# A 32-row form of an expert's last block in a mixture-of-experts kernel

## Chip, core and metric

The kernel runs on one core of a Trainium2 chip. The metric is the device time of one execution in microseconds (us). Engines are named as in the profile: PE (matmul; PEld is its weight load, PEq or PEldq its instruction sequencer), DVE, ACT, POOL, SP. L1120 is line 1120 of the kernel before.

## What is computed

The reference is a two-layer network in fp32: an RG-LRU mixer with a mixture-of-experts (MoE) layer over 1,280 tokens (1,024 and 256 of context), then a differential attention with a second MoE layer over 1,024 tokens. The change is in the MoE. Each token goes to 2 of 32 experts, and an expert is

```
yb = (silu(x @ w_gate[e]) * (x @ w_up[e])) @ w_down[e]     # 1024 -> 512 -> 1024
out[token] += yb * weight[token]
```

The routing of the drawn inputs gives these tokens per expert, in the order in which the kernel takes the experts. Layer 0: 105, 63, 87, 113, 56, 75, 60, 153, 36, 76, 44, 105, 123, 89, 97, 69, 40, 40, 55, 153, 18, 49, 19, 107, 24, 102, 125, 41, 140, 82, 37, 177. Layer 1: 75, 80, 14, 6, 26, 274, 40, 43, 7, 246, 4, 7, 49, 43, 34, 14, 15, 170, 0, 8, 1, 133, 5, 92, 16, 284, 9, 16, 129, 146, 0, 62. In blocks of 64 rows, with one block at least, that is 54 blocks in each layer.

## The kernel before

`moe` (from L1033) is called once for each layer. An expert's weights are six chunks of 1 MB (two of gate, two of up, two of down), loaded by SP's queue through `load` into a ring of 20 buffers (`raws`); a load waits until PE has read what the buffer held, and is left out where an expert has no tokens (`used`). POOL gathers each block's token rows (`fetch`, `gather`) and scatters the results (`y_out`).

A block of up to 64 rows has four steps on PE. `gate_up` (L1114): 16 fp32 matmuls of 512 columns, two at a time on the two 64-column tiles of the array, one for gate and one for up; the profile shows each as two records, 32 in all. ACT then takes SiLU of the one half, and DVE multiplies it by the other into `hm`. `x_t` (L1109) transposes the rows of the next block through `p_x` into `xt`. `down` (L1131) is the down projection of the block *before*: 8 matmuls (16 records) into `p_y`, which `y_out` scales on ACT into `ym` and scatters from POOL. `h_t` (L1125) transposes this block's `hm` into `ht`. So PE does gate_up of a block, x_t of the next, down of the last and h_t, over and over.

The number of blocks is only known on the chip. `nblk` holds it for each expert (L1023, L1024), and each engine loads it into a register (`count`, L1152). The program is written out for five blocks of each of the 32 experts, one inside the other (`finish`, L1190): `tc.If(n > b + 1)` at L1193 goes into the next block, its Else ends the expert, and the engine jumps past the parts that it doesn't need. This branch stands behind gate_up on every engine. On PE a branch hint (`expect`) is given ahead of gate_up; it names the Else as the likely target. The branch has no other work than the jump, but PE's code must be at hand: a DMA queue (q8 in the profile) brings it in packets of 16 KB.

## Time and profile before

| | us |
|---|---|
| median of 3 runs (lowest, highest) | 3120.76 (3112.51, 3124.94) |
| profiled execution, its span | 3128.07, 3126.5 |
| mean granted clock of TensorE | 0.946 |
| MoE of layer 0 (from 613.7 to 1300.1 us of the span) | 686.4 |
| MoE of layer 1 (from 2358.1 to 3064.1 us) | 706.0 |

The busy time of an engine is the sum of its instructions; a row of a group gives line, engine, operation, the tiles that it writes and reads, and after the bars its busy time, the mean of one and the idle time of the engine just before it, with what ended most of that. "issue" is idle time for which the profile shows no other engine as the cause. The granted clock is a share of 2.4 GHz.

### The profile page before, as it was taken

The page shows a single profiled execution, that of the slowest core. Times are in us where ns is not written, and L with a number is a line of the kernel's source. Part 1 is how long each engine was busy: PE and PEld are TensorE (multiplying, and loading weights), DVE is VectorE, ACT ScalarE, POOL GpSimd, SP SyncE. Part 2 cuts the span into 40 slices and gives each one's busy share as a digit, 9 for nine tenths or more (in the row PEclk, how much of TensorE's full clock was granted, in tenths as well). Part 3 has the DMA queues.
Part 4 walks back from the last instruction along what each step waited for, and adds up shares of the span by engine and source line. Part 5 has one row for each costly group of instructions (what it writes and reads, how often), then busy time and mean ns, then how long its engine had stood idle before and what let it go on. Part 6 is the DMA issues. An engine that isn't in the chain of part 4 may idle for free. (4 is left out here: it accounts for less than half of the span.)

```text
span 3126.5 us, 40919 instructions
## 1 busy us (share of the span) xinstructions
PE 2770.1 (89%) x14542; PEld 1709.2 (55%) x14542; DVE 1374.5 (44%) x2597; ACT 964.4 (31%) x1813; POOL 532.8 (17%) x756
## 2 busy tenths in 40 slices
PE   5999989699999999658999999997977989999991
PEld 3667768433333333257888888886862333333330
DVE  6566676511111111297666666666771111111115
ACT  4566642100011001245454544545420101001011
POOL 2121101211111111140110111100021111112113
PEclk8999989799999999879999999998988999999996
DMA  5556465588879987450000000003255786888544
GB/s 199 160 176 207 161 210 183 195 318 352 342 288 357 377 325 277 149 189 23 26 27 6 26 26 27 6 7 135 105 216 224 313 350 268 346 345 350 196 155 179
DMA packets 175212, 611.49 MB, mean 196 GB/s; under 512 B 28488, under 2 KB 81504, under 8 KB 127104
## 3 DMA queue, kind: packets, MB, share of 16 engines
q1 hardware_dynamic: 133872, 493.85, 41.4%
q0 software_dynamic: 39936, 111.52, 9.9%
q8 instruction: 217, 3.56, 0.5%
q14 instruction: 275, 2.25, 0.2%
q10 hardware_dynamic: 912, 0.32, 0.0%
HBM read 560.23 MB, written 64.22 MB: 200 GB/s over the span
## 5 line engine op out<-in xcount | busy, mean ns | idle before, releaser
L1120 PE MATMUL p_g<-wr,xt 128*64 128x512 f32 x3456 | 775.8, 600 | 40.6 <-ACT ym L1142 32.1
L1120 PEld LDWEIGHTS p_g<-wr,xt 128*64 128x64 f32 x3456 | 268.5, 138 | 465.1 <-issue 413.9
L1123 DVE TENSOR_TENSOR hm<-act,p_g 64x512 f32<-64x512 f32 x108 | 74.7, 692 | 839.7 <-ACT act L1122 804.9
L1136 PE MATMUL p_y<-wr,ht 128*64 128x512 f32 x1728 | 412.6, 610 | 19.4 <-issue 18.1
L1122 ACT ACTIVATE act<-p_g 64x512 f32<-64x512 f32 x108 | 63.6, 589 | 798.2 <-PE p_g L1120 768.5
L1136 PEld LDWEIGHTS p_y<-wr,ht 128*64 128x64 f32 x1728 | 118.6, 138 | 229.2 <-issue 214.2
L56 PE MATMUL qkv<-qwh,hth 128*128 128x384 f32 (+1 forms) x640 | 216.2, 338 | 2.0 <-ACT hth L1439 1.1
L57 PE MATMUL qkv<-qwh,htl 128*128 128x384 f32 (+1 forms) x640 | 210.1, 328 | 0.9 <-DVE htl L1444 0.9
L58 PE MATMUL qkv<-qwl,hth 128*128 128x384 f32 (+1 forms) x640 | 209.4, 327 | 0.6 <-DVE qwl L1294 0.6
L1534 DVE TENSOR_REDUCE st<-sc 128x1 f32<-128x1280 f32 x128 | 190.2, 1486 | 22.0 <-PE sc L1521 20.4
L1129 DVE COPY ht<-p_h 128x256 f32<-128x256 f32 x108 | 45.9, 425 | 342.1 <-PE p_h L1128 336.4
L1537 ACT ACTIVATE wide<-sc,st 128x1280 f32<-128x1280 f32 x128 | 168.9, 1325 | 68.7 <-DVE st L1534 68.6
L1560 PE MATMUL po<-V,wide 128*128 128x128 f32 x1280 | 167.2, 288 | 1.5 <-ACT wide L1554 0.5
L1560 PEld LDWEIGHTS po<-V,wide 128*128 128x128 f32 x1280 | 156.7, 201 | 13.4 <-ACT wide L1554 12.6
L1105 POOL DMA_INDIRECT wide<-h2d,tabs x108 | 112.2, 1039 | 280.8 <-issue 79.6
L1554 ACT COPY wide<-wtp 128x512 f32<-128x512 f32 (+1 forms) x192 | 87.8, 522 | 199.9 <-PE wtp L1553 199.7
L1566 POOL DMA_DIRECT2D od<-ot x56 | 30.4, 542 | 625.2 <-ACT ot L1563 625.2
L1142 ACT ACTIVATE ym<-p_y,cur 128x512 f32<-128x512 f32 x64 | 44.0, 688 | 285.0 <-PE p_y L1136 233.5
L1518 PE MATMUL sc<-KT,QS 128*128 128x512 f32 (+1 forms) x384 | 117.2, 393 | 15.3 <-ACT KT L1368 11.8
L1112 PEld LDWEIGHTS p_x<-ident,wide 128*128 128x128 f32 x432 | 60.9, 210 | 122.9 <-issue 97.8
L1144 POOL DMA_INDIRECT yd<-ym,tabs x44 | 44.0, 1000 | 491.0 <-POOLq L1193 309.4
L56 PE MATMUL o<-wh,sth 128*128 128x512 f32 x288 | 118.9, 413 | 7.4 <-DVE xres L810 5.1
(354 smaller groups left out, 4652.7 us busy)
## 6 DMA issues: line engine op xcount, KB each, us to landing
wr<-in_moe_w_gate_dram SPq DMA_DIRECT2D x124, 1024.0 KB
wr<-in_moe_w_up_dram SPq DMA_DIRECT2D x124, 1024.0 KB
wr<-in_moe_w_down_dram SPq DMA_DIRECT2D x124, 1024.0 KB
wm<-in_w_mod_dram POOLq DMA_DIRECT2D x80, 512.0 KB
cy<-yd SPq DMA_DIRECT2D x26, 512.0 KB
qraw<-in_da_w_qkv_dram SPq DMA_DIRECT2D x48, 256.0 KB
xd<-xres POOLq DMA_DIRECT2D x18, 512.0 KB
h2d<-h POOLq DMA_DIRECT2D x18, 512.0 KB
```

Of the source, the lines that this page charges most:

```text
L56: nc.tensor.matmul(ps, lh, rh, start=start, stop=False)
L57: nc.tensor.matmul(ps, ll, rh, start=False, stop=False)
L58: nc.tensor.matmul(ps, lh, rl, start=False, stop=stop)
L1105: nc.gpsimd.indirect_dma_start(out=dst, out_offset=None, in_=h2v, in_offset=bass.IndirectOffsetOnAxis(ap=idx, axis=0), bounds_check=2 * N ...
L1120: nc.tensor.matmul(p_g[i * B:(i + 1) * B, :], xt[:, j, h * B:(h + 1) * B], w[i][:, j, :], start=(h == 0 and j == 0), stop=(h == 1 and j == ...
L1123: nc.vector.tensor_tensor(hm[B:], act[B:], p_g[B:], OP.mult)
L1136: nc.tensor.matmul(p_y[h * B:(h + 1) * B, :], ht[:, 2 * c + j, :], w[:, j, h * 512:h * 512 + 512], start=(c == 0 and j == 0), stop=(c == 1 ...
L1518: nc.tensor.matmul(o, qs[:, half, :], KT[b][:, half, c0:c0 + n], start=True, stop=False)
L1534: nc.vector.tensor_reduce(st[:, half:half + 1], sc_[:, half, :], AX.X, OP.max)
L1537: nc.scalar.activation(p, sc_[:, half, :], AF.Exp, bias=st[:, 2 + half:3 + half], scale=0.125, accum_out=st[:, 4 + half:5 + half])
L1554: nc.scalar.copy(wT[:, g * 4:g * 4 + n, :], pt[:, 0:n, :])
L1560: nc.tensor.matmul(po[:, 0:P], wT[:, k, :], V[h % 2][:, k, :], start=(k == 0), stop=(k == TT - 1))
```

## The change

An expert's rows are now counted in quarters of 32 (`nq`, at least one: `n1`), and where their number is odd and at most ten, the last block holds only 32 rows (`odd`). In front of each block's gate_up stands a new branch, `full`; its Else takes the quarter:

- `gate_up_q`: 32 matmuls of 256 columns with 32 rows each, four at a time on the four 32-column tiles of the array (two for gate, two for up). The moving columns are taken as pairs, 8 of every 16 bytes.
- `h_t_q`: two transposes in the place of four.
- `down_q`: 16 matmuls of 256 columns on four tiles; it runs inside the *next* expert's first block, behind a branch on `odds[e]`, with `down` in the other arm (`give`).
- `cur_q`: eight small operations of POOL in the place of one copy; `y_out` then scatters 128 rows of 1 KB.

The old branch, `more`, stands behind the full gate_up as before. The hint for the next `full` is given in `turn`, and the hint for `more` at the head of the full arm. By the counts above, 36 of the 108 blocks become quarters: 12 in layer 0 (3 of experts with one block, 6 with two, 3 with three) and 24 in layer 1 (16 with one block, two of them without tokens; 3 with two, 3 with three, 2 with five).

```diff
-        nc.vector.tensor_scalar(nblk, ct[:, :E], float(B - 1), None, op0=OP.add)
-        nc.vector.tensor_scalar(nblk, nblk, 6, None, op0=OP.arith_shift_right)
+
+        nq, n1, odd, nb = (nblk[:, i, :] for i in range(4))
+        nc.vector.tensor_scalar(nq, ct[:, :E], float(Q - 1), None, op0=OP.add)
+        nc.vector.tensor_scalar(nq, nq, 5, None, op0=OP.arith_shift_right)
+        nc.vector.tensor_scalar(n1, nq, 1.0, None, op0=OP.max)
+        nc.vector.tensor_scalar(nb, n1, 1.0, None, op0=OP.add)
+        nc.vector.tensor_scalar(odd, nb, 1, None, op0=OP.arith_shift_right)
+        nc.vector.tensor_scalar(nb, odd, 1.0, None, op0=OP.mult)
+        nc.vector.scalar_tensor_tensor(odd, odd, 2.0, n1, op0=OP.mult, op1=OP.subtract)
+        nc.vector.scalar_tensor_tensor(odd, n1, 2.0 * NB64 + 0.5, odd, op0=OP.is_lt, op1=OP.mult)
...
+        def gate_up_q(e):
+
+            for h in range(2):
+                w = [chunk(e, 2 * i + h, 4).rearrange("p j (q f) -> p j q f", f=4) for i in range(2)]
+                for j in range(4):
+                    for i in range(2):
+                        for c in range(2):
+                            o = slice((2 * i + c) * Q, (2 * i + c + 1) * Q)
+                            nc.tensor.matmul(p_g[o, 0:2 * P].rearrange("t (q f) -> t q f", f=2),
+                                             xt[:, j, h * B:h * B + Q], w[i][:, j, :, 2 * c:2 * c + 2],
+                                             start=(h == 0 and j == 0), stop=(h == 1 and j == 3),
+                                             tile_position=(0, (2 * i + c) * Q))
+            nc.scalar.activation(act[B:, 0:2 * P], p_g[:B, 0:2 * P], AF.Silu)
+            nc.vector.tensor_tensor(hm[B:, 0:2 * P], act[B:, 0:2 * P], p_g[B:, 0:2 * P], OP.mult)
+
+        def h_t_q():
+            hv = hm[B:, 0:2 * P].rearrange("t (q f) -> t f q", f=2)
+            for f in range(2):
+                nc.tensor.transpose(p_h[:, f, :], hv[:, f, :], ident[B:, B:])
+            nc.vector.tensor_copy(ht.rearrange("p (c f) b -> p f c b", f=2)[:, :, :, 0:Q],
+                                  p_h[:, 0:2, :].rearrange("p f (c r) -> p f c r", r=Q))
+
+        def down_q(e):
+            for c in range(2):
+                w = chunk(e, 4 + c, 2)
+                for j in range(2):
+                    for m in range(4):
+                        nc.tensor.matmul(p_y[m * Q:(m + 1) * Q, 0:2 * P], ht[:, 2 * c + j, 0:Q],
+                                         w[:, j, m * 2 * P:(m + 1) * 2 * P], start=(c == 0 and j == 0),
+                                         stop=(c == 1 and j == 1), tile_position=(0, m * Q))
+
+        def cur_q(cur, t):
+
+            for h in range(2):
+                for s in range(2):
+                    dst = cur[h * B + s * Q:h * B + (s + 1) * Q]
+                    frm = t[h * B:h * B + Q]
+                    nc.gpsimd.tensor_scalar(dst[:, 1:2], frm[:, 1:2], 2.0, float(s), op0=OP.mult, op1=OP.add)
+                    nc.gpsimd.tensor_copy(dst[:, 2:3], frm[:, 2:3])
...
-        def y_out(cur):
-            ym = yms[len(scat) % 2]
-            nc.scalar.activation(ym, p_y, AF.Copy, scale=cur[:, 2:3].bitcast(F32))
+        def y_out(cur, quarter=False):
+            n = 2 * P if quarter else F
+            ym = yms[len(scat) % 2][:, 0:n]
+            nc.scalar.activation(ym, p_y[:, 0:n], AF.Copy, scale=cur[:, 2:3].bitcast(F32))
             nc.gpsimd.memset(spacer, 0.0)
-            si = nc.gpsimd.indirect_dma_start(out=ydv, out_offset=bass.IndirectOffsetOnAxis(ap=cur[:, 1:2], axis=0),
-                                              in_=ym, in_offset=None, bounds_check=4 * N - 1, oob_is_err=False)
+            si = nc.gpsimd.indirect_dma_start(out=ydq if quarter else ydv,
+                                              out_offset=bass.IndirectOffsetOnAxis(ap=cur[:, 1:2], axis=0),
+                                              in_=ym, in_offset=None, bounds_check=(8 if quarter else 4) * N - 1,
+                                              oob_is_err=False)
...
-        def turn(xb, e, cur):
-
+        def give(e, cur, quarter):
+
+            if e < 0:
+                return
+            if quarter is None:
+                with tc.If(odds[e] > 0) as one:
+                    down_q(e)
+                    y_out(cur, True)
+                with one.Else():
+                    down(e)
+                    y_out(cur)
+            else:
+                down(e)
+                y_out(cur)
+
+        def turn(xb, e, cur, quarter, nxt=None):
+
+            if nxt is not None:
+                expect("full", *nxt)
             if xb is not None:
                 x_t(xb)
-            if e >= 0:
-                down(e)
-                y_out(cur)
-            h_t()
-
-        def expect(e, b):
-
-            tc.mark_branch_hint_location(f"more{l}_{e}_{b}", "LikelyTaken",
-                                         (mybir.EngineType.PE,))
-
-        def finish(e, b, prev):
+            give(e, cur, quarter)
+
+        def expect(what, e, b):
+
+            tc.mark_branch_hint_location(f"{what}{l}_{e}_{b}", "LikelyTaken", (mybir.EngineType.PE,))
+        def block(e, b, prev):
...
+            then = (e + 1, 0) if e + 1 < E else None
+            with tc.If(n > 2 * b + 1, label=f"full{l}_{e}_{b}") as full:
+                expect("more", e, b)
+                gate_up(e)
+                with tc.If(n > 2 * b + 2, label=f"more{l}_{e}_{b}") as more:
+                    if b + 1 < NB64:
+                        if b + 2 < NB64:
+                            fetch(e, b + 2)
+                        turn(rows_of(e, b + 1), *prev, (e, b + 1))
+                        h_t()
+                        block(e, b + 1, (e, tab(e, b), False))
...
+                with more.Else():
+                    turn(nxt, *prev, then)
+                    h_t()
+                    nc.gpsimd.tensor_copy(curs[e % 2], tab(e, b))
+            with full.Else():
+                gate_up_q(e)
+                turn(nxt, *prev, then)
+                h_t_q()
+                cur_q(curs[e % 2], tab(e, b))
...
-            n = count(ORDER[e])
+            n = count(ORDER[e], 1)
+            odds[e] = count(ORDER[e], 2)
             know(e + 5)
-            expect(e, 0)
-            gate_up(e)
             fetch(e + 1, 1)
             fetch(e + 2, 0)
-            finish(e, 0, (e - 1, curs[(e - 1) % 2]))
+            block(e, 0, (e - 1, curs[(e - 1) % 2], None))
             for k in ([] if e == 0 else [6 * e - 2, 6 * e - 1]) + list(range(6 * e, 6 * e + 4)):
                 load(k + NM)
-        down(E - 1)
-        y_out(curs[(E - 1) % 2])
+        give(E - 1, curs[(E - 1) % 2], None)
```

How this moves PE's instructions shows at two places. The first is the seam between an expert's last block and the next expert's gate_up, in layer 0. Before (`p_h` is h_t, `nblk` the load of the block count, `p_g` gate_up; a TENSOR_LOAD is the register load):

```order
L1128 MATMUL p_h<-ident,hm 128x64 [waits DVE_49]
L1128 MATMUL p_h<-ident,hm 128x64 x3
L1193 UNCONDITIONAL_BRANCH [waits PE_sequencer_49]
L1173 UNCONDITIONAL_BRANCH
L1739 BRANCH_PREFETCH_HINT
L1093 UNCONDITIONAL_BRANCH x4
L1152 TENSOR_LOAD nblk
L1120 MATMUL p_g<-wr_4647,xt 64x512 [waits DMAHW4_49,DVE_49,Activation_49]
```

The same seam now, behind the quarter arm of the expert before it (L1143 is gate_up_q, L1122 x_t, L1153 h_t_q, L1130 gate_up, L1260 the branch `full`):

```order
L1153 MATMUL p_h<-ident,hm 128x64 [waits DVE_49]
L1153 MATMUL p_h<-ident,hm 128x64
L1260 UNCONDITIONAL_BRANCH [waits PE_sequencer_49]
L1226 UNCONDITIONAL_BRANCH
L1103 UNCONDITIONAL_BRANCH x4
L1205 TENSOR_LOAD nblk x2
L1260 COMPARE_AND_BRANCH
L1814 BRANCH_PREFETCH_HINT
L1130 MATMUL p_g<-wr_4653,xt 64x512 [waits DMAHW4_49,DVE_49,Activation_49]
```

A second register load and the `full` branch now stand between an expert's last transposes and the next gate_up, and the hint ahead of gate_up is now that of `more`.

The second place is the quarter arm of the second expert of layer 0, at its head (the first row ends the arm before it; the hint is that of the next expert's `full`):

```order
L1263 UNCONDITIONAL_BRANCH [waits PE_sequencer_49]
L1814 BRANCH_PREFETCH_HINT
L1143 MATMUL p_g<-wr_4653,xt 32x256 [waits DVE_49,DMAHW4_49,Activation_49]
L1143 MATMUL p_g<-wr_4653,xt 32x256
L1143 MATMUL p_g<-wr_4654,xt 32x256 [waits DMAHW5_49]
```

and further on in it, where x_t is followed by both forms of down (L1234 is the branch on `odds`, L1162 down_q, L1186 down):

```order
L1122 MATMUL p_x<-ident,wide_89 128x128 x3
L1234 COMPARE_AND_BRANCH
L1162 MATMUL p_y<-wr_3237,ht 32x256 [waits DMAHW0_49]
L1162 MATMUL p_y<-wr_3237,ht 32x256 x7
L1162 MATMUL p_y<-wr_3238,ht 32x256 [waits DMAHW1_49]
L1162 MATMUL p_y<-wr_3238,ht 32x256 x7
L1234 UNCONDITIONAL_BRANCH
L1186 MATMUL p_y<-wr_3237,ht 64x512 [waits DMAHW0_49]
```

The hint has moved to the head of the quarter arm, right behind the place to which `full` jumps, and each of the three ways out of an expert's first gate_up carries both forms of down. Over the whole program PE's rows grow from 19336 to 29972.

## Rows read from the trace of the kernel before

**Rows 1.** The page: the span, and busy time by engine.
```profile
span 3126.5 us, 40919 instructions
...
PE 2770.1 (89%) x14542; PEld 1709.2 (55%) x14542; DVE 1374.5 (44%) x2597; ACT 964.4 (31%) x1813; POOL 532.8 (17%) x756
```

**Rows 2.** Busy time by stretch: the two MoE stages; columns as in the first line.
```profile
core 0: us, PE busy (x) PEld busy (x) DVE busy (x) ACT busy (x) POOL busy (x), PEclk, DMA share, GB/s
...
613.70:1300.10 686.40, 654.35 (x3020) 251.76 (x3020) 97.11 (x162) 69.75 (x109) 117.11 (x190) 0.99 0.79 309
...
2358.10:3064.10 706.00, 663.66 (x3020) 254.36 (x3020) 96.97 (x161) 69.65 (x109) 116.89 (x190) 0.98 0.72 283
```

**Rows 3.** The page's costliest groups: gate_up and down; count, busy us, mean ns.
```profile
L1120 PE MATMUL p_g<-wr,xt 128*64 128x512 f32 x3456 | 775.8, 600 | 40.6 <-ACT ym L1142 32.1
...
L1136 PE MATMUL p_y<-wr,ht 128*64 128x512 f32 x1728 | 412.6, 610 | 19.4 <-issue 18.1
```

**Rows 4.** Timeline of PE, layer 1, single-block experts: start, us, group, idle before.
```profile
2427.54 7.09 PE L1120 MATMUL p_g<-wr,xt 128*64 128x512 f32 x32 [0.56 <-ACT ym L1142]
2434.55 0.75 PE L1112 MATMUL p_x<-ident,wide 128*128 128x128 f32 x4
2435.24 3.65 PE L1136 MATMUL p_y<-wr,ht 128*64 128x512 f32 x16
2438.82 0.69 PE L1128 MATMUL p_h<-ident,hm 64*128 64x64 f32 x4
2440.08 7.09 PE L1120 MATMUL p_g<-wr,xt 128*64 128x512 f32 x32 [0.56 <-ACT ym L1142]
2447.09 0.75 PE L1112 MATMUL p_x<-ident,wide 128*128 128x128 f32 x4
```

**Rows 5.** Waits of the weight queue (SP), layer 1: total us, times, longest.
```profile
SPq L684 <- PE p_y L1136: 384.4, 47, 53.3
```

**Rows 6.** Timeline of PE around 406 us: a matmul on four 32-column tiles.
```profile
406.09 1.07 PE L147 MATMUL mps<-wm,cs 128*32 128x256 f32 x16
407.09 0.39 PE L56 MATMUL ps_y<-hth,wh 128*128 128x256 f32 x1
```

**Rows 7.** The page's groups: PE's weight loads with contiguous columns, and with every fourth column.
```profile
L1560 PEld LDWEIGHTS po<-V,wide 128*128 128x128 f32 x1280 | 156.7, 201 | 13.4 <-ACT wide L1554 12.6
...
L1112 PEld LDWEIGHTS p_x<-ident,wide 128*128 128x128 f32 x432 | 60.9, 210 | 122.9 <-issue 97.8
```

**Rows 8.** Busy time by stretch, where the DMA engines are full (columns as in Rows 2).
```profile
2425.00:2470.00 45.00, 43.31 (x206) 17.12 (x204) 5.85 (x10) 4.52 (x7) 11.19 (x17) 1.00 1.02 411
```

**Rows 9.** Lines 1024 and 1220: a block-count operation and the copy of cur.
```profile
L1024 DVE TENSOR_SCALAR nblk<-nblk x2: 181/181/181, 599.0 to 2346.2; 128x32 int32<-128x32 int32 x2
...
L1220 POOL COPY cur<-tabs x64: 187/202/235, 639.2 to 3061.4; 128x3 int32<-128x3 int32 x64
```

**Rows 10.** Line 1152, 2436 to 2437 us: the block count loaded for that expert.
```profile
L1152 PEldq TENSOR_LOAD <-nblk x1: 309/309/309, 2436.3 to 2436.3; - x1
```

**Rows 11.** Line 1193, PE's sequencer: compare-and-branch, ns min/median/max, whole run.
```profile
L1193 PEldq COMPARE_BRANCH  x136: 69/302/5992, 618.8 to 3051.3; - x136
```

**Rows 12.** Line 1193, 2442 to 2443 us: one branch of a single-block expert.
```profile
L1193 PEldq COMPARE_BRANCH  x1: 3467/3467/3467, 2442.7 to 2442.7; - x1
```

**Rows 13.** DMA, 2423 to 2461 us: the queue that brings PE's code; packets, MB, share.
```profile
q8 instruction: 6, 0.10, 1.1%
```

**Rows 14.** Line 1193, 668 to 669 us: last branch of a two-block expert.
```profile
L1193 PEldq COMPARE_BRANCH  x1: 332/332/332, 668.6 to 668.6; - x1
```

**Rows 15.** Timeline of PE, layer 0, 645 to 653 us: a stop inside down.
```profile
645.94 1.93 PE L1136 MATMUL p_y<-wr,ht 128*64 128x512 f32 x6
650.12 2.73 PE L1136 MATMUL p_y<-wr,ht 128*64 128x512 f32 x10 [2.25 <-issue]
```

**Rows 16.** Waits of PE, layer 1: total us, times, longest.
```profile
PE p_y L1136 <- issue: 10.7, 4, 2.8
PE p_x L1112 <- issue: 7.6, 6, 5.1
```

More of the change, by code (lines that the diff above doesn't have):

```diff
@@ L46 @@
 B = P // 2
+Q = P // 4
 NB64 = 5
@@ L96, in model @@
     nc.vector.tensor_scalar(ie, ie.bitcast(I32), 1.0 / 64.0, None, op0=OP.mult)
-    nblk = const.tile([P, E], I32, name="nblk")
+    nblk = const.tile([P, 4, E], I32, name="nblk")
     wide = [const.tile([P, UO], F32, name=f"wide{i}") for i in range(3)]
@@ L1072, in moe @@
         rows = {}
+        odds = {}
         h2v = h2d[l][0:N, :].rearrange("n (h d) -> (n h) d", h=2)
-        ydv = yd[l][0:2 * N, :].rearrange("n (h d) -> (n h) d", h=2)
+        ydv, ydq = (yd[l][0:2 * N, :].rearrange("n (h d) -> (n h) d", h=h) for h in (2, 4))
         def tab_load(j0, j1, queues):
@@ L1148, in y_out, with count @@
             scat.append(si)
-        def count(e, engines=None):
+        def count(e, what, engines=None):
             kw = {} if engines is None else {"engines": engines}
-            return nc.values_load(nblk[0:1, e:e + 1], min_val=0, max_val=N // B,
+            return nc.values_load(nblk[0:1, what, e:e + 1], min_val=0, max_val=N // (B if what == 3 else Q),
                                   skip_runtime_bounds_check_because="an expert has at most N tokens", **kw)
@@ L1157, in know @@
             if e < E:
-                used[e] = count(ORDER[e], (mybir.EngineType.SP,))
-                rows[e] = count(ORDER[e], (mybir.EngineType.Pool,))
+                used[e] = count(ORDER[e], 0, (mybir.EngineType.SP,))
+                rows[e] = count(ORDER[e], 3, (mybir.EngineType.Pool,))
         def tab(e, b):
@@ new lines, in turn @@
+            give(e, cur, quarter)
+        def expect(what, e, b):
+            tc.mark_branch_hint_location(f"{what}{l}_{e}_{b}", "LikelyTaken", (mybir.EngineType.PE,))
+        def block(e, b, prev):
+            nxt = rows_of(e + 1, 0) if e + 1 < E else None
+            then = (e + 1, 0) if e + 1 < E else None
[9 more added lines that the diff above has]
+                        block(e, b + 1, (e, tab(e, b), False))
+                    else:
+                        turn(None, *prev)
+                        h_t()
+                        nc.gpsimd.tensor_copy(curs[2], tab(e, b))
+                        with tc.For_i(NB64, count(ORDER[e], 3), 1) as j:
+                            for h in range(2):
+                                nc.gpsimd.dma_start(flat[h * B:(h + 1) * B, 0, :], slotd[l][0:E * N, :].rearrange(
+                                    "(j p e) c -> j p e c", e=E, p=B)[bass.ds(j, 1), :, ORDER[e], :].rearrange(
+                                        "o p c -> (o p) c"))
+                            halve(flat)
+                            gather(xms[0], flat[:, 0, 0:1])
+                            x_t(xms[0])
+                            gate_up(e)
+                            give(e, curs[2], False)
+                            h_t()
+                            nc.gpsimd.tensor_copy(curs[2], flat[:, 0, :])
+                        if nxt is not None:
+                            x_t(nxt)
+                        nc.gpsimd.tensor_copy(curs[e % 2], curs[2])
+                with more.Else():
+                    turn(nxt, *prev, then)
+                    h_t()
+                    nc.gpsimd.tensor_copy(curs[e % 2], tab(e, b))
[4 more added lines that the diff above has]
+                cur_q(curs[e % 2], tab(e, b))
```

28 lines of the change are left out of this document (removed).

## Prediction

> **What bounds the kernel now.** I read the busy times first. PE is busy for 89% of the span [rows 1], and in the two MoE stages for 654 of 686 us and 664 of 706 us, at a granted clock of 0.99 and 0.98 of 2.4 GHz [rows 2]. The groups say with what: gate_up holds 776 us and down 413 us of the whole span [rows 3]. The 3456 records of gate_up are 32 for each of 108 blocks. The timeline then shows one block: gate_up begins at 2427.54, x_t at 2434.55, down at 2435.24, h_t at 2438.82, the next gate_up at 2440.08 [rows 4]. That is 7.01 + 0.69 + 3.58 + 0.69 us, and 0.56 us of waiting at a new expert: 12.54 us. The next candidate is the weight traffic. The DMA engines are busy at a share of 0.79 and 0.72 in these stages [rows 2], but SP, which starts the loads, waits 384 us in layer 1 for PE to release buffers [rows 5]: weights are early, PE is late. So what PE saves in the MoE shortens the kernel until the weights, or something behind them, come last.
>
> **Term 1, the quarter's matmuls.** gate_up's 32 records run two at a time: 16 pairs in 7.01 us, 0.438 us for a pair of 512 columns. gate_up_q has 64 records of 256 columns, 16 sets of four. If four tiles run together at the same column rate, a set takes 0.219 us and gate_up_q 3.5 us. The trace has such matmuls elsewhere: 16 records with 128x32 weights and 256 columns start at 406.09 and the next matmul at 407.09 [rows 6], so four sets in 1.00 us, 0.25 us each, its ends included; by that gate_up_q takes 4.0 us. It saves 3.0 to 3.5 us. down_q has 8 sets, 1.75 to 2.0 us against 3.58, and saves 1.6 to 1.8. Two transposes in the place of four save 0.3. In all 4.9 to 5.6 us for each quarter; I take 5.3, towards the first rate, since 64 records have fewer ends than 16. Times 36 quarters: **191 us** (176 to 202), 64 of it in layer 0.
>
> gate_up_q reads its columns as 8 of every 16 bytes. No row shows a matmul that does so. The nearest is a weight load: of every fourth column, for x_t, it takes 210 ns, of contiguous columns 201 ns [rows 7]. I take it as free; the other end is half the rate, 3.5 us for each quarter, and is a rival below.
>
> **Term 2, the weights.** Where the DMA engines are full they move 411 GB/s [rows 8]. Six chunks are 6.29 MB, 15.3 us. A single-block expert takes 12.54 us of PE now and 7.2 with a quarter, so a run of such experts lives on the ring's 20 buffers, 3.3 experts. Walking the list of experts with 11.9 us for a full block, 6.6 for a quarter and 2.55 us for a chunk, layer 0 never runs dry, and layer 1 (16 of its quarters are alone in their expert) waits some 15 to 25 us in all: **+20 us**.
>
> **Term 3, the small work.** `nblk` takes seven more DVE operations for each layer at 0.18 us [rows 9], ahead of everything that reads a count: **+2 us**. cur_q's eight operations at the 0.2 us of today's copy [rows 9] are 1.4 us more of POOL for each quarter. `cur` is only read when the next expert's down has ended, at least a gate_up and a down later (5 us), and POOL is busy 117 of 686 us [rows 2]: nothing; uncovered it would be 1.4 x 36 = 50 us. The shorter SiLU and product hide under x_t and down as today. The second register load costs PE's sequencer 0.31 us an expert [rows 10]. It is covered: the load at 2436.3 stands ahead of a gate_up that starts at 2440.08, so the sequencer is 3.8 us ahead of PE there. Without that cover it is 64 x 0.31 = 20 us.
>
> **Term 4, the branches.** This is the term that decides, and the trace of before doesn't show it directly. PE's 136 branches at line 1193 take 69 ns to 5992 ns, with a median of 302 [rows 11]. In the single-block expert above, the branch at 2442.7 took 3467 ns [rows 12] although a hint stood 6.4 us in front of it, beside the load at 2436.3 [rows 10]. It cost nothing: it stands behind gate_up, the sequencer had run ahead, and x_t began at 2447.09, right where gate_up ended [rows 4]. Three such experts in a row fetch six packets of code in 38 us [rows 13], two for each expert, one in 6.3 us. In a two-block expert, whose hint comes a whole block earlier, the last branch took 332 ns [rows 14]. And when the code runs on into a packet that isn't there, PE stops in the middle of down for 2.25 us [rows 15]; layer 1 has such stops of 10.7 us in p_y and 7.6 us in p_x [rows 16].
>
> The Trainium skill, "Runtime: NRT & Kernel Launch", section "Instruction fetch mechanics", says that a taken branch to a target outside the sequencer's current two-page window has to wait for that page to be fetched, and that this makes runtime control flow expensive. The 3467 ns agree, the 332 ns after an early hint don't. By that rule alone each jump into or past a quarter arm is a stall, and the sum below would go to its dear end.
>
> The change moves the decision to where there is the least cover: `full` stands *ahead* of gate_up, behind the last transposes of the block before, and its Else lies behind five nested blocks. The hint for it stands at the head of a quarter arm, right behind a jump, when the queue is still busy with the arm's own code.
>
> - 19 quarters that are alone in their expert: a jump of 3.5 us [rows 12] to 6.0 us [rows 11] against a lead of 3.8 us less the extra load after a full block, perhaps half that after a quarter, whose matmuls last half as long. Visible: 1 us to all of the 5.3 us saved, where two packets for each expert at 6.3 us apiece hold it to the old 12.5 us. I take 3.2, nearer to the miss than to the hit, since the rows of single-block experts show misses: +61 us.
> - 17 quarters behind full blocks: the hint comes a block ahead, which is the row of 332 ns, but the arm's second half is new code [rows 15] and the way out jumps past the arms of the blocks around it. 0 to 4 us, I take 2 (about one stop as in rows 15): +34 us.
> - 28 experts whose last block is full: `more` is covered by gate_up as today, but the end now jumps over the quarter's code. 0 to 3 us, I take 1: +28 us.
>
> Together **+123 us** (19 to 253). Some of it falls into layer 1's waits for weights and isn't paid twice: **-15 us**.
>
> **The sum.** 3128 - 191 + 20 + 2 + 123 - 15 = 3067 us for the profiled execution, which lay 7 us above the median of the runs shown: **3060 us**, 2% faster. A measurement of this kernel can tell about 0.5% (16 us) from no change.
>
> **The rivals.**
> - *The hints work everywhere, the branches are hidden.* For it: the 332 ns. Against: single-block experts miss today with a hint some 6 us ahead. Term 4 falls to about 30 us, with less of it under the weights' waits: 3128 - 191 + 20 + 2 + 30 - 5, less 7, gives 2977 us.
> - *Code fetch eats the gain: slower.* One mechanism, at the `full` branch and the arms behind it: each expert needs two or three packets where two came in 12.5 us, and PE stands at the seam until they are there. The gain without branches is 191 - 20 - 2 = 169 us over 64 experts, so it decides where they lose more than 2.6 us on average. With 3.3 us (a 3.5 us miss that is hardly covered) it is 211 us, some 15 under weights' waits: 3128 - 169 + 211 - 15, less 7, gives 3148 us. For it: the 6.3 us of a packet and the stops in down. The rule of "Runtime: NRT & Kernel Launch" in term 4 points this way. Against: full blocks still give cover, and they are the majority.
> - *The quarter isn't half as long*: columns in pairs, or four tiles that don't overlap, give 3.5 us for each quarter back (126 us). A longer quarter hides about a third of term 4 (40 us) and term 2's 20: 3060 + 126 - 60 = 3126 us. Against it: rows 6 and 7.
> - *The weights become the bound of layer 1*: the ring is emptied more often than by my walk, +40 us, 3100 us.
>
> **How the numbers follow.** My forecast has 0.56, the hidden branches 0.16, the slower case 0.17, the longer quarter 0.06, the weights 0.05. My forecast's own range is 3010 to 3110, by term 4 between 70 and 175 us. The range of 8 in 10 takes in most of the first rival and part of the second: 2975 to 3145. Faster by over 0.5% means below 3105: 0.52 of the forecast, the hidden branches and most of the weights: 0.71. Within 0.5%: 0.04 of the forecast, most of the longer quarter and the lower part of the slow case: 0.12. Slower: 0.17.
>
> **What would show it.** In the profile after, gate_up_q should take 3.5 to 4.0 us from its start to x_t (7 would be the third rival), and down_q 1.75 to 2.0. The `full` branch of PE should show a bimodal time, a few hundred ns or 3.5 to 6 us, with the idle time in front of gate_up and gate_up_q; if nearly all are short, the first rival holds. The queue of PE's code should carry more packets than two for each expert [rows 13]. The stages should shrink by 20 to 40 us each; layer 1's, with twice the quarters, not by twice layer 0's. SP's wait for PE should fall, and PE should wait for weights in layer 1 alone. I am wrong if the stage times move while the branches are all short, or if PE's granted clock falls where it waits, of which the stages of before show nothing at 0.98 and more.

## The result: 5% slower, and the profile after

The changed kernel takes 3279.22 us in the median (3271.66 to 3279.32, 4 runs) against 3122.85 us for the kernel before on the same chip: a ratio of 1.0496 (95% interval 1.0474 to 1.0519). I had forecast 3060 us, 2% faster. The page of the changed kernel (line 1130 is now gate_up, 1143 gate_up_q, 1186 down, 1162 down_q, 1122 x_t):

```profile
span 3277.7 us, 46026 instructions
...
PE 2676.6 (82%) x16198; PEld 1715.5 (52%) x16198; DVE 1362.3 (42%) x2609; ACT 949.4 (29%) x1813; POOL 577.0 (18%) x1008
...
q8 instruction: 282, 4.62, 0.6%
...
L1130 PE MATMUL p_g<-wr,xt 128*64 128x512 f32 x2304 | 550.4, 629 | 85.4 <-issue 58.5
...
L1143 PE MATMUL p_g<-wr,xt 128*32 128x256 f32 x2304 | 167.4, 443 | 99.3 <-issue 82.5
...
L1122 PE MATMUL p_x<-ident,wide 128*128 128x128 f32 x432 | 87.2, 328 | 135.8 <-DMA wide<-h2d,tabs 100.8
```

PE's busy share fell from 89% [rows 1] to 82%. The 36 quarters are there: 2304 records of gate_up_q are 64 for each. But the idle time in front of PE's groups is 85 us for gate_up, 99 us for gate_up_q and 136 us for x_t. Of the last, 101 us are waits for gathered token rows; the kernel before had 23 us of them, in two stops at the heads of the stages. By stretch, the two MoE stages (columns as in rows 2):

```profile
608.00:1379.50 771.50, 632.58 (x3576) 256.93 (x3576) 92.93 (x163) 64.62 (x109) 133.31 (x276) 0.91 0.72 276
2439.90:3215.20 775.30, 591.69 (x4128) 253.63 (x4128) 87.96 (x162) 59.50 (x109) 147.09 (x360) 0.87 0.66 259
```

They answer to [rows 2]. The stages took 686 and 706 us and take 772 and 775: the whole loss lies in them. PE is busy 22 and 72 us less, where I had worked out 64 and 127, and the granted clock fell from 0.99 and 0.98 to 0.91 and 0.87. So there are three things to explain: stops of PE for code ("issue"), waits for rows, and a lower clock.

A stretch of layer 1 shows all three. Its experts have one quarter each (timeline of PE, and the granted clock, the last but two number, in one down_q):

```profile
2499.03 3.89 PE L1143 MATMUL p_g<-wr,xt 128*32 128x256 f32 x64 [0.58 <-DVE ht L1154]
2509.82 1.13 PE L1122 MATMUL p_x<-ident,wide 128*128 128x128 f32 x4 [6.91 <-DMA wide<-h2d,tabs]
2510.88 3.64 PE L1162 MATMUL p_y<-wr,ht 128*32 128x256 f32 x32
2514.45 0.45 PE L1153 MATMUL p_h<-ident,hm 64*128 64x64 f32 x2
2516.61 3.90 PE L1143 MATMUL p_g<-wr,xt 128*32 128x256 f32 x64 [1.70 <-issue]
2528.04 1.13 PE L1122 MATMUL p_x<-ident,wide 128*128 128x128 f32 x4 [7.53 <-DMA wide<-h2d,tabs]
```

```profile
2510.90:2514.40 3.50, 3.50 (x33) 1.36 (x32) 0.69 (x1) 0.00 (x0) 0.00 (x0) 0.50 1.01 414
```

gate_up_q takes 3.9 us, as worked out. But from one x_t to the next are 18.2 us, where a whole 64-row expert took 12.54 [rows 4], and after a stop of 6.9 us down_q runs at a granted clock of 0.50, the level of 1.2 GHz, and takes 3.64 us instead of the 1.93 of an undisturbed one (run 1 below). POOL in the same stretch:

```profile
2501.86 1.10 POOL L1115 DMA_INDIRECT wide<-h2d,tabs  x1 [4.14 <-PE p_g L1143]
2507.10 0.09 POOL L1194 MEMSET spacer<- 1x1 f32 x1 [4.14 <-issue]
2508.56 1.02 POOL L1195 DMA_INDIRECT yd<-ym,cur  x1 [1.37 <-DMA yd<-ym,tabs]
2509.65 0.18 POOL L1172 TENSOR_SCALAR cur<-tabs 32x1 int32<-32x1 int32 x1
...
2510.16 0.18 POOL L1173 COPY cur<-tabs 32x1 int32<-32x1 int32 x1
2515.95 0.19 POOL L1172 TENSOR_SCALAR cur<-tabs 32x1 int32<-32x1 int32 x1 [5.61 <-POOLq L1260]
...
2516.68 0.18 POOL L1173 COPY cur<-tabs 32x1 int32<-32x1 int32 x1
2520.80 1.10 POOL L1115 DMA_INDIRECT wide<-h2d,tabs  x1 [3.94 <-PE p_g L1143]
```

cur_q's first four operations follow the scatter of 2508.56. The fifth starts only at 2515.95, some 7.4 us after that scatter was issued, and the next gather only at 2520.80. The profile names POOL's own sequencer as what ended this wait (POOLq L1260). But in the order of POOL's instructions the fifth operation carries a wait for all eight semaphores of POOL's DMAs, that of the scatter just issued among them, in some 190 of the program's 320 quarter arms, and for most of the eight in the others. The gather lands at about 2528, and x_t waits for it. Before, the copy of `cur` waited for two of these at most. POOL is also idle for 4 us behind the jump into a new arm ("issue", the row of 2507.10), though its branches themselves take some 40 ns. In front of these `spacer` operations such stops are 182 us in 62 places; before they were 95 us in 33. POOL seems to wait for its code as PE does; no run tries that apart.

**Theory P** is this chain: POOL's wait for the scatter, the late gather, PE's wait for rows. **Theory F** is code fetch on the sequencers: jumps at seams, arms that push the code apart, and the new branches. Its signs are there too: the queue of code carries 282 packets (217 before), and single passes of the branch `full` take as long as I had expected of a miss, though most are short (line 1260, PE's sequencer; ns min/median/max):

```profile
L1260 PEldq COMPARE_BRANCH  x125: 69/81/6105, 609.1 to 3193.9; - x125
```

### The profile page after: what moved, and what is told of

It reads as the page before. It is cut to its first block, busy times and chain, and to the rows that moved or that the text cites. A ratio compares the mean times of both kernels' runs of the same rounds, so it can differ in the third digit from the quotient of the medians.

```text
span 3277.7 us, 46026 instructions
## 1 busy us (share of the span) xinstructions
PE 2676.6 (82%) x16198; PEld 1715.5 (52%) x16198; DVE 1362.3 (42%) x2609; ACT 949.4 (29%) x1813; POOL 577.0 (18%) x1008
## 5 line engine op out<-in xcount | busy, mean ns | idle before, releaser
L1130 PE MATMUL p_g<-wr,xt 128*64 128x512 f32 x2304 | 550.4, 629 | 85.4 <-issue 58.5
L1130 PEld LDWEIGHTS p_g<-wr,xt 128*64 128x64 f32 x2304 | 187.0, 144 | 393.6 <-issue 362.7
L1133 DVE TENSOR_TENSOR hm<-act,p_g 64x512 f32<-64x512 f32 x72 | 49.8, 692 | 652.6 <-ACT act L1132 628.3
L1186 PE MATMUL p_y<-wr,ht 128*64 128x512 f32 x1152 | 283.8, 638 | 22.9 <-issue 11.6
L1143 PE MATMUL p_g<-wr,xt 128*32 128x256 f32 x2304 | 167.4, 443 | 99.3 <-issue 82.5
L1132 ACT ACTIVATE act<-p_g 64x512 f32<-64x512 f32 x72 | 42.4, 589 | 558.1 <-PE p_g L1130 545.9
L1122 PE MATMUL p_x<-ident,wide 128*128 128x128 f32 x432 | 87.2, 328 | 135.8 <-DMA wide<-h2d,tabs 100.8
L1122 PEld LDWEIGHTS p_x<-ident,wide 128*128 128x128 f32 x432 | 63.1, 210 | 211.2 <-issue 140.6
L1143 PEld LDWEIGHTS p_g<-wr,xt 128*32 128x32 f32 x2304 | 87.0, 122 | 165.2 <-issue 130.6
L1186 PEld LDWEIGHTS p_y<-wr,ht 128*64 128x64 f32 x1152 | 82.4, 145 | 171.6 <-issue 160.1
L1193 ACT ACTIVATE ym<-p_y,cur 128x256 f32<-128x256 f32 (+1 forms) x64 | 36.3, 568 | 408.5 <-PE p_y L1186 124.8
```

What stands on the lines that cost most here:

```text
L1122: nc.tensor.transpose(p_x[:, j, :], xv[:, j, :], ident)
L1130: nc.tensor.matmul(p_g[i * B:(i + 1) * B, :], xt[:, j, h * B:(h + 1) * B], w[i][:, j, :], start=(h == 0 and j == 0), stop=(h == 1 and j == ...
L1143: nc.tensor.matmul(p_g[o, 0:2 * P].rearrange("t (q f) -> t q f", f=2), xt[:, j, h * B:h * B + Q], w[i][:, j, :, 2 * c:2 * c + 2], start=(h ...
L1186: nc.tensor.matmul(p_y[h * B:(h + 1) * B, :], ht[:, 2 * c + j, :], w[:, j, h * 512:h * 512 + 512], start=(c == 0 and j == 0), stop=(c == 1 ...
```

## The experiments

Each ratio is against the kernel before, run on the same chip, with its 95% interval.

**1. cur_q on DVE.**

```diff
-                    nc.gpsimd.tensor_scalar(dst[:, 1:2], frm[:, 1:2], 2.0, float(s), op0=OP.mult, op1=OP.add)
-                    nc.gpsimd.tensor_copy(dst[:, 2:3], frm[:, 2:3])
+                    nc.vector.tensor_scalar(dst[:, 1:2], frm[:, 1:2], 2.0, float(s), op0=OP.mult, op1=OP.add)
+                    nc.vector.tensor_copy(dst[:, 2:3], frm[:, 2:3])
```

> cur_q's eight small operations move from POOL to DVE; nothing else changes. Theory P (POOL's chain): after the change the fifth of these operations waits for the scatter issued just before it, so POOL issues the next gather some 7 us late and PE waits 101 us for gathered rows in x_t. Then this wait falls below 30 us here, most of it in layer 1, and the time falls from 3279 to 3170-3215 us, ratio to the kernel before 1.015-1.03. Theory F (code fetch on PE's and POOL's sequencers alone): the rows come earlier, but PE then stands at its own jumps; the time stays above 3230 us, ratio 1.035-1.05.

3195.61 us, 1.0222 (1.0205 to 1.0239). Theory P's numbers came: x_t waits 23 us for rows in place of 101, as before the change (waits of PE: total, times, longest; first before, then the changed kernel, then this one):

```profile
PE p_x L1112 <- DMA wide<-h2d,tabs: 23.2, 2, 13.0
...
PE p_x L1122 <- DMA wide<-h2d,tabs: 100.8, 22, 13.1
...
PE p_x L1122 <- DMA wide<-h2d,tabs: 23.0, 2, 12.9
```

Layer 0, with few lone quarters, didn't move; layer 1 did (by stretch, columns as in rows 2):

```profile
611.60:1385.20 773.60, 632.84 (x3576) 257.18 (x3576) 102.42 (x259) 64.53 (x109) 115.70 (x180) 0.91 0.71 276
2441.50:3139.10 697.60, 567.37 (x4128) 246.40 (x4128) 107.36 (x354) 59.41 (x109) 112.75 (x168) 0.91 0.74 288
```

POOL's wait is worth 1.0496 - 1.0222 = 0.027, 86 us. That is net of a small new wait: gate_up and gate_up_q stand 24 us for cur_q on DVE. What is left, I put down to theory F. The same experts as above, timeline of PE:

```profile
2507.64 0.75 PE L1122 MATMUL p_x<-ident,wide 128*128 128x128 f32 x4
2508.32 1.93 PE L1162 MATMUL p_y<-wr,ht 128*32 128x256 f32 x32
2510.19 0.44 PE L1153 MATMUL p_h<-ident,hm 64*128 64x64 f32 x2
2515.57 5.81 PE L1143 MATMUL p_g<-wr,xt 128*32 128x256 f32 x64 [4.93 <-issue]
```

x_t now follows at once, and the stop has moved to the seam: 4.93 us for the jump of `full`, and behind it a gate_up_q of 5.81 us where 3.8 would do, at a granted clock of 0.63.

**2. No quarter is ever taken.**

```diff
+        nc.vector.tensor_scalar(n1, nb, 2.0, None, op0=OP.mult)
         nc.vector.scalar_tensor_tensor(odd, odd, 2.0, n1, op0=OP.mult, op1=OP.subtract)
```

> The number of quarters is rounded up to an even one, so no expert ever takes a quarter arm; all branches, hints and arms of the change stay in the program and 108 full blocks run as before the change. Theory F in the form 'a larger program and later hints cost all experts': ratio to the kernel before 1.015-1.04 (about 1-2 us for each of 64 experts), with PE idle as issue in p_g and p_x. Theory F in the form 'only the jumps into quarter arms cost', and theory P (cur_q is never run): 1.000-1.008.

3314.34 us, 1.0625 (1.0595 to 1.0655), more than either form had allowed: the branches and arms cost 195 us though nothing ever jumps into a quarter. Where, from this kernel's profile (gate_up is its line 1131, the branch `more` its line 1264; first the page's group, then PE's passes of line 1264 from 2640 to 2684 us, then the packets of code from 2642 to 2704 us):

```profile
L1131 PE MATMUL p_g<-wr,xt 128*64 128x512 f32 x3456 | 822.3, 626 | 152.9 <-issue 120.5
```

```profile
L1264 PEldq COMPARE_BRANCH  x7: 506/1792/3586, 2642.0 to 2681.3; - x7
```

```profile
q8 instruction: 11, 0.18, 1.2%
```

gate_up waits 120.5 us as "issue"; of the 40.6 us in front of it before, 32.1 were ACT's [rows 3]. Two of line 1264's passes belong to each expert: the branch behind gate_up, and the jump past the quarter arm at its end. The stretch holds some four experts with one full block each, and 11 packets are nearly three for each, where the kernel before took two [rows 13]. That is one packet in 5.6 us, against one in 6.3 before. It isn't the most that the queue can bring: in the same run five came within 20 us (3228.9 to 3249.1).

**3 and 4. The arms chosen when the kernel is built,** from the known counts, with cur_q on POOL and on DVE. This is no kernel for other inputs; it shows the matmuls without branches.

```diff
-            with tc.If(n > 2 * b + 1, label=f"full{l}_{e}_{b}") as full:
+            if last_q(e) == b:
+                gate_up_q(e)
+                turn(nxt, *prev)
+                h_t_q()
+                cur_q(curs[e % 2], tab(e, b))
+                return
```

> The arms are chosen when the kernel is built, from the known token counts: a quarter's arm stands there without the branches full and odds, the blocks that would follow it are not in the program, and full blocks keep the branch more with its hint ahead of gate_up. cur_q stays on POOL. Theory F: all lost time was fetch, so the whole gain of the matmuls appears: 2945-2985 us, ratio 0.945-0.957. Theory P: where cur_q still waits for the scatter, x_t waits for rows; 2990-3060 us, ratio 0.96-0.98. If four tiles or columns in pairs were slow: gate_up_q 7 us and a ratio near 0.98 without waits.

> As the kernel with arms chosen at build time, and cur_q on DVE. Both theories: neither far jumps nor POOL's wait are left, so this is the ceiling of the idea: 2930-2975 us, ratio 0.94-0.953, PE busy in the two MoE stages down by about 190 us, granted clock above 0.95, and weights the only wait of layer 1 (15-25 us). A ratio above 0.97 would say that a third cause, the weights or the clock, holds the gain back.

2995.6 us, 0.9588 (0.9572 to 0.9604), and 2934.45 us, 0.9398 (0.9382 to 0.9414). The first lies between what the two theories expected; the second, at the very edge of its range, is 191 us below the kernel before. The 61 us between them are POOL's wait again: x_t waits 91 us for rows in the first and 27 in the second. By stretch, the second, and its wait for weights in layer 1:

```profile
610.30:1234.70 624.40, 590.66 (x3576) 243.87 (x3576) 102.81 (x259) 64.64 (x109) 115.82 (x180) 0.99 0.86 339
2290.00:2869.70 579.70, 542.29 (x4128) 234.24 (x4128) 107.67 (x354) 59.51 (x109) 113.06 (x168) 0.98 0.86 343
```

```profile
PE p_g L1143 <- DMA wr<-in_moe_w_up_dram: 8.3, 4, 2.5
```

These are the same 3576 and 4128 matmul records as in the changed kernel, which held PE for 632.58 and 591.69 us there. So the changed kernel loses 91 us to the lower clock and 251 us to idle time of PE. The clock isn't a cause of its own: it stays at 0.99 and 0.98 where PE isn't stopped. Against the kernel before [rows 2], PE is busy 185 us less in the two stages of this run and idle 3 us less.

**5 to 7. The hint, and the order of the arms** (all with cur_q on DVE). Without the hint for `full`; then also with the quarter arm first; then with this arm for lone quarters only (`odd` is set only where an expert has one quarter, and deeper blocks have no branch `full`).

```diff
-            if nxt is not None:
-                expect("full", *nxt)
```

```diff
-            with tc.If(n > 2 * b + 1, label=f"full{l}_{e}_{b}") as full:
+            with tc.If(n < 2 * b + 2, label=f"full{l}_{e}_{b}") as full:
+                gate_up_q(e)
...
+            with full.Else():
```

> As the kernel with cur_q on DVE (ratio 1.022), without the hint for the branch full; the hint for more stays. If this hint brings the quarter arm's code in time for some experts (my prediction took it so for the 17 quarters behind full blocks), the time rises by 17 x 2 to 3.5 us: ratio 1.033-1.042. If the hint is lost because the code queue is busy behind each jump: ratio 1.018-1.026, the idle time of gate_up_q as before it.

> As without the full hint, with the arms of the branch full changed round: the quarter arm stands first and is reached by falling through, the full arm is reached by a short jump over it, an expert's last full block runs out without a jump over a quarter arm, and a quarter ends with the far jump. Theory F1 (each unhinted far jump at a seam costs 2 to 4 us, wherever it stands): quarters keep their loss, the 28 experts that end in a full block lose theirs (about 2.5 us each): ratio 0.995-1.01. Theory F2 (the queue of code, one packet in 6 us, is the bound, and the arms' length decides): 1.015-1.03, idle time only moves.

> Quarter arm first, and only for experts whose whole work is one quarter (19 of 36 quarters); the deeper blocks have no branch full, no odds and no quarter arm. Ideal gain 19 x 5.2 = 99 us. F1: 19 far jumps at about 3.5 us less lead cost 50 us, and 45 experts pay a short jump: ratio 0.975-0.995. F2: the shorter program needs fewer packets: 0.97-0.985, and the packets of code per stage come back to about 75.

3248.66 us, 1.0413 (1.0395 to 1.0431): the hint is worth 60 us, as expected if it brings the arm's code for some experts. It shows in front of gate_up_q (waits of PE, run 1, then without the hint):

```profile
PE p_g L1143 <- issue: 95.8, 21, 9.1
...
PE p_g L1143 <- issue: 160.9, 30, 10.1
```

3286.12 us, 1.0535 (1.0513 to 1.0558), and 3256.52 us, 1.0429 (1.0412 to 1.0447): both outside what I had expected, and in no theory's favour. In the last, the longest stops are those of the full block behind a lone quarter (waits of PE in layer 1: total, times, longest):

```profile
PE p_g L1130 <- issue: 97.5, 14, 11.2
```

The longest of them take 8 to 11 us, while a single pass of a branch takes at most 7.25 us in this run. There the quarter's far jump is followed at once by the jump over the next expert's quarter arm, so I read it as two fetches in a row; that wasn't tried apart.

**8. The quarter in down alone.** gate_up and h_t are full, there is no branch `full`, and ACT writes the four quarters of p_y into the full layout of `ym`, so that `cur` and the scatter are those of the kernel before.

```diff
+                for m in range(4):
+                    h, s = m // 2, m % 2
+                    nc.scalar.activation(ym[h * B:h * B + Q, s * 2 * P:(s + 1) * 2 * P], p_y[m * Q:(m + 1) * Q, 0:2 * P],
+                                         AF.Copy, scale=cur[h * B:h * B + Q, 2:3].bitcast(F32))
```

> Only the down projection knows the quarter: gate_up, h_t and the branch more are those of the kernel before, down_q and down stand behind the short branch on odds, ACT writes the four quarters of p_y into the full layout of ym (four small operations for one), and cur and the scatter are as before the change. Ideal gain 36 x 1.75 = 63 us. If the short branch is free, as the rows of line 1234 after the change suggest (median 208 ns): ratio 0.98-0.985. If its extra code (32 more matmul records at each of two exits of the first block) costs an expert 1 us: ratio 1.0.

3148.97 us, 1.0078 (1.0057 to 1.01). The 63 us of down_q are gone and 25 more: the short branch on `odds`, which I had left out of my sum, costs some 88 us, ACT's small operations included. PE's waits as "issue" in front of its MoE groups are 79 us here and 31 before, half of them in front of the two forms of down.

**9 and 10. Taking the all-full kernel apart:** without the quarter arms (the Else of `full`), and then without the branch on `odds` too.

```diff
-            with full.Else():
-                gate_up_q(e)
-                turn(nxt, *prev, then)
-                h_t_q()
-                cur_q(curs[e % 2], tab(e, b))
```

> As the kernel in which all blocks are full (ratio 1.0625, no quarter ever taken), with the quarter arms taken out of the program; the branch full (always fallen through), its hints and the short branch on odds with both forms of down stay. If the 189 us of that kernel were the jump at each expert's end over the quarter arms and the code that these arms push apart: ratio 1.005-1.03. If the branch full, its hints and odds cost them: it stays at 1.045-1.06.

> As the kernel without quarter arms, and without the branch on odds: down alone. What is left of the change is the branch full, fallen through, a hint for it, and the hint for more just ahead of its gate_up. If odds costs what the down-only kernel suggests (25 us more than before although it should have gained 63): 60-90 us below the kernel without quarter arms, ratio 0.995-1.01. If the later hint for more is the cost: 1.01-1.03.

3215.53 us, 1.0294 (1.0265 to 1.0322), and 3130.71 us, 1.0029 (1.0013 to 1.0045). So the branch `full`, where it is fallen through, and the late hint for `more` cost 9 us net, `odds` 83 us, and the arms 103 us. These differences hold more than the branches. In both kernels ACT loads its function table 63 times more, 1.28 us each in front of SiLU, and x_t waits longer for rows. Summed over PE's groups of the MoE, its waits as "issue" are 31 us before, 5 in run 10, 30 in run 9 and 172 in run 2; x_t's waits for rows are 23, 62, 48 and 23. So the 9 us are 38 us more of waiting for rows, less 27 us of "issue". From run 10 to run 9 only 25 us are "issue"; 22 us are waits for ACT, 18 for weights, and PE is busy 26 us longer. And the 103 us are 142 us of "issue" with less waiting for rows, ACT and weights. The branch on `odds` in the first of them (line 1235, PE's sequencer; ns min/median/max):

```profile
L1235 PEldq COMPARE_BRANCH  x64: 222/450/6493, 641.5 to 3143.4; - x64
```

Its median is harmless, but some passes take 6 us, and it stands ahead of down, which waits 29.9 us in run 9 and 1.2 in run 10.

**11 and 12. The whole change with ACT's four operations in the place of cur_q and the second scatter,** in both layers, and in layer 1 only.

```diff
-                cur_q(curs[e % 2], tab(e, b))
+                nc.gpsimd.tensor_copy(curs[e % 2], tab(e, b))
```

> The whole change with its hints, but ACT writes the four quarters of p_y into the full layout of ym (four small operations), so cur and the scatter are as before the change and POOL has no work of the quarter's own. Theory P: the waits for gathered rows go as with cur_q on DVE, and DVE's and POOL's extra operations too: ratio 1.005-1.022. If ACT's four operations come onto the path (p_y is released later, gate_up waits for ym): 1.022-1.035.

> The same in layer 1 only, where two thirds of the quarters are; layer 0 has the branches and the blocks of the kernel before. With cur_q on DVE layer 1 took 698 us against 708 before, layer 0 774 against 688. So layer 0 should come back to 688 and the whole to 3095-3120 us, ratio 0.99-1.0. Below 0.99 the version would beat both kernels.

3194.67 us, 1.0227 (1.0208 to 1.0247): at the border between what I had expected of theory P and of a cost on ACT, and the same as with cur_q on DVE. POOL's wait is gone by either way, and nothing more is to be had there. 3112.13 us, 0.9979 (0.9961 to 0.9998): layer 1 alone just pays, by 0.2%.

**13 to 16. The quarter in gate_up and h_t alone.** down always takes 64 rows; rows beyond 32 are stale and their indices lie outside the scatter's bound. No `odds`, no cur_q. In both layers; in layer 1; in layer 1 for lone quarters only; in both layers with the branch at an expert's first two blocks only.

```diff
             ym = yms[len(scat) % 2]
-            if quarter is None:
-                with tc.If(odds[e] > 0) as one:
-                    down_q(e)
-                    evac(ym, cur, True)
-                with one.Else():
...
+            down(e)
+            evac(ym, cur)
```

> Quarters in gate_up and h_t alone: down always takes 64 rows (those beyond 32 are stale and fall out of the scatter by their indices), so there is no branch on odds, no cur_q and no second scatter. Ideal gain 36 x 3.5 = 126 us, given back 10 (branch full, hints) and 100 (arms in the program) and some 70 for jumps into the arms, by the differences measured so far. If the parts add: 3155-3185 us, ratio 1.01-1.02. If the parts are not independent (fewer packets of code also make the other jumps cheaper): 0.985-1.005.

> The same in layer 1 only, layer 0 as in the kernel before. Against the whole change with ACT's four operations in layer 1 (0.998): 24 x 1.75 = 42 us lost in down, about 45 us won by leaving odds out. If the parts add: ratio 0.993-1.002. If the branch on odds costs less where quarters run: above 1.005.

> Layer 1 only, and only the first block of an expert may be a quarter (16 of 24 there): one arm for each expert in place of five. Ideal gain 16 x 3.5 = 56 us. If the arms cost by their number in the program (length of the jumps, packets of code): they cost a fifth to a third of before, and 15-35 us are won, ratio 0.988-0.996. If each passing of a branch and its merge costs, whatever the length: the 16 experts with full blocks pay as before, ratio 0.997-1.006.

> As the kernel with the quarter in gate_up and h_t alone (0.992), but the branch full and its arm stand only at an expert's first two blocks, two arms for each expert in place of five: 28 of the 36 quarters are left, 28 us of gain are given up. If what an expert pays grows with the arms that its jumps cross and the code that they add: 30 to 60 us come back, ratio 0.982-0.992. If each passing of a branch and its merge costs, whatever the length of the program, only the deep blocks save it: 0.993-1.002.

3107.7 us, 0.9919 (0.9891 to 0.9947): this version beats both kernels. 3109.6 us, 0.9934 (0.9916 to 0.9952). 3118.72 us, 0.9973 (0.996 to 0.9986). 3149.7 us, 1.0094 (1.0072 to 1.0116). The first, from its page and by stretch, and the last by stretch:

```profile
q8 instruction: 249, 4.08, 0.5%
...
L1143 PE MATMUL p_g<-wr,xt 128*32 128x256 f32 x2304 | 168.1, 443 | 85.3 <-issue 76.5
```

```profile
611.80:1300.40 688.60, 624.14 (x3384) 251.71 (x3384) 92.77 (x163) 67.10 (x109) 118.09 (x192) 0.97 0.79 309
2356.80:3044.20 687.40, 597.90 (x3744) 248.91 (x3744) 87.89 (x162) 64.54 (x109) 117.78 (x191) 0.94 0.75 292
```

```profile
612.20:1313.30 701.10, 635.57 (x3294) 251.92 (x3294) 94.19 (x163) 67.74 (x109) 118.13 (x192) 0.97 0.78 303
2369.60:3084.20 714.60, 615.60 (x3594) 251.93 (x3594) 90.05 (x162) 65.60 (x109) 117.87 (x192) 0.93 0.72 280
```

The parts don't add: against experiment 11 it gives up 63 us of down's gain and is 96 us faster, so with quarters running `odds` and what hangs on it (down_q, ACT's four operations) cost some 160 us, not 83. PE's waits as "issue" fall with it from 206 us to 116. The stops of gate_up_q are still there, 76.5 us. The last run is a miss, above both of its ranges: with two arms for each expert in place of five, PE was busy 29 us longer, for the 8 quarters given up (28 us expected), and idle 11 us *longer* too. So it isn't simply the number of arms in the program that an expert pays for. Each branch and merge that it passes is nearer, and fits the third run, but it doesn't explain 1.0094 either. Nor do the packets of code. Their number goes with the cost of the branches elsewhere (206 in run 10, 217 before, 249 in run 9, 282 in run 1, 329 in run 5), but run 16 has 242 of them and is slower than run 13 with 249.

## Why the prediction was wrong

The parts as shares of the time before, in us of 3123. They add up because the fifth row takes the rest; the second to fourth come from kernels without quarters, with the other waits that runs 9 and 10 hold:

| part | from | us |
|---|---|---|
| the quarters' matmuls, no branch | run 4 | -188 |
| `full` fallen through, late hint, net | run 10 | +9 |
| branch on `odds`, no quarter taken | 9 less 10 | +83 |
| quarter arms in the program, none taken | 2 less 9 | +103 |
| jumps into the arms, and what doesn't add | 1, less the four above | +62 |
| cur_q on POOL | after less 1 | +86 |
| sum | after | +155 |

- *Term 1, the matmuls* (-191): right. gate_up_q takes 3.8 to 3.9 us from its start to x_t, down_q 1.87, and in run 4 PE is busy 185 us less in the two stages. Columns in pairs cost nothing to speak of: a set of four takes 0.24 us in gate_up_q and 0.23 in down_q, whose columns lie together. So four tiles run together.
- *Term 2, the weights* (+20): too dear. Run 4 has the whole gain, at a DMA share of 0.86. PE waits 8.3 us in front of gate_up_q for them in layer 1, some 10 us in all.
- *Term 3, the small work*: **failed at cur_q**, which I put at nothing and, uncovered, at 1.4 us of POOL for each quarter. I priced what the operations take and not what they wait for, nor who is queued behind them. The wait for the last scatter held back the next gather; with cur_q off POOL 86 us come back (run 1), and run 11, which does without cur_q, takes the same time.
- *Term 4, the branches*: **failed in size, and one part was missing.** The branch on `odds` stood in the order that I quoted and had no term at all; it costs 83 us or more. An expert that ends in a full block and passes the arms pays 1.6 us in run 2 (103 us over 64 experts), where I had taken 1. In the changed kernel only 28 experts end so, and how its loss divides between them and the jumps into the arms isn't shown: the two are 165 us together, against 28 and 95 in my sum. In all 257 us against 123, before the 15 us that I took off for an overlap with the weights' waits; these are some 10 us even in run 4.
- *The cover.* I took a few us of sequencer lead as cover for each stop by itself, and the 6.3 us between two packets [rows 13] as what a packet costs. But the queue can be faster: the kernel before itself brings four within 20 us (3040.4 to 3060.6). Nearly three packets for each expert came where two had come (run 2), and I read it so that a stop uses up the lead of the next; no run shows that by itself. I gave the dear end of my sum too little weight. The Trainium skill, "Runtime: NRT & Kernel Launch", section "Instruction fetch mechanics", says that a taken branch out of the window waits for its page. Run 2 agrees, where passing line 1264 takes up to 3.6 us in the stretch shown.
- *The clock*: I named its fall as what would prove me wrong, and put it at nothing from [rows 2]. It makes 91 us of the loss, as a follower of the stops.
- *The slower rival* had the mechanism (code fetch at the seams), a chance of 0.17 and 3148 us. It was the right one of the rivals, without POOL's part: run 1, which has none, takes 3196 us. Its 3.3 us for each expert came to about 4 (257 us over 64).

What stays open: why the parts of the fetch don't add, why the branch on `odds` costs twice as much where quarters run, and why fewer arms did not help in run 16. That the stops are waits for code is read from the passes of the branches and from the packets; no run changes the fetch alone, and only the hint comes near it (run 5). Where the arms' code falls on the packets' borders may decide it; it wasn't tried.

## What to carry to other kernels

A branch in front of the work that it chooses can be paid by everyone who passes it, also by those who don't take it (run 2: 195 us with no quarter taken): price the jump past the other arm, every small branch, and the code that both arms add, by a run in which the branch is there and never taken. Price each new small operation by the wait that it brings and by what is queued behind it on its engine, not by its own time. And of a split that helps two steps, try each step alone: here gate_up alone, with two thirds of the gain and without the branch on `odds`, is 0.8% faster than before; both together, with POOL's wait taken away, are 2% slower.

## What the chip showed that I had not expected

- A hint at the head of an arm, right behind a jump, is not lost: without the hints for `full` the kernel loses 60 us, and gate_up_q's stops grow from 96 to 161 us (run 5). I had thought the queue too busy for it. How much of this the hints give that stand a block ahead, isn't shown.
- A stop of PE can be paid twice: at 2510.90 to 2514.40 the granted clock was 0.50 after 6.9 us of idle time, and down_q took 3.64 us instead of 1.93.
- POOL's branches take 40 ns by their own rows, but POOL stood still for some 4 us behind a jump into a new arm (4.14 us before 2507.10, "issue").
